# A hybrid encoder block on one core: small products in joint runs, decay rows per head, earlier scan loads, buffers moved by 32 bytes

## The chip, the cores and the metric

The kernel runs on one core of a Trainium2 chip. Its time is the device time of one execution in microseconds. The kernel before took 1745.05 us (median of three runs, 1745.01 to 1745.94).

## The reference

One block with two branches over x of 512 tokens by 2048 features, all in float32. What matters of it, in short:

```python
n = rmsnorm(x, norm_w)
proj = n @ w_in                       # 2048 -> 13376 columns, split into:
# g_qkv, g_z, g_beta, g_a (gated DeltaNet), m_qk, m_v, m_o, m_z, m_i, m_f (mLSTM), gates
# branch A, 8 heads of 128, both directions: conv of width 5 + silu, l2norm of q and k, then by chunks
decay = exp(where(causal, gc[:, None] - gc[None, :], -inf))
sol = triangular_solve(lower(kb @ k.T * decay) + I, [v * beta, kb * exp(gc)])
v_new = u - w @ state                                   # the scan over chunks, one state per head
state = state * exp(g_last) + k_dec.T @ v_new
out = (q * exp(gc)) @ state + (q @ k.T * decay) @ v_new
# branch B, 8 heads of 128, both directions: stabilised mLSTM by chunks, with a running maximum m
c = f * c + i * k.T @ v ; h = (w_inter * q @ c + scores @ v) / max(|den|, exp(-m))
merged = sigmoid(gates_a) * (y_a @ w_branch_gdn) + sigmoid(gates_b) * (y_b @ w_branch_mlstm)
return rmsnorm(x + merged @ w_out, final_norm_w)
```

## The kernel before, in words

**Large products.** Every weight matrix is cut into units. A unit of `w_in` is 128 output columns: two blocks of 24 products of 128x128 by 128x512. Float32 accuracy comes from a split in two parts: ACT casts the raw weights `wr` to `wh` (L168), DVE subtracts to get `wl` (L169), and a block does 16 products that alternate between `nth` and `ntl` (high and low part of the normed input) against `wh`, and 8 of `nth` against `wl`. The input part is the moving operand. SP issues the loads of `wr` (L159), four blocks ahead at most; the splits are two blocks ahead. The units follow each other in a fixed order: k, q and v of eight GDN heads (`gk`, `gq`, `gv`), their gates `gz`, the merge gates `mg0` to `mg27`, five units for each mLSTM head (`m0` to `m4`), `mg28` to `mg31`, then the branch matrices `br` (moving operand `yh` and `yl`, the split branch outputs), then `w_out` (moving operand `wh` and `wl`). 6560 products are large ones.

**Small products.** All else is written as one generator, `master`. After every fourth large product it is advanced by one step (a tick), up to its next `yield`. So the places of the yields decide between which large products the small ones fall on PE. `master` runs `setup` (gate sums, decay), `gdn_pre` for each head (scores `pgm` and transposes `px`, stored to DRAM), `gdn_solve` (a triangular solve on DVE for all heads, then two copies that transpose it on ACT, L570 and L574), the scan `gdn_head` of eight heads, two at a time (`rolling`), `ml_head` for eight heads, and the split of the branch outputs. The 1008 small products are of float32 and take two instructions each, transposes one.

**Order.** Each engine works through a fixed list in order; an instruction that waits holds up what stands behind it. SP issues nearly all transfers, weights and small ones, from one list. In `setup`, the decay of all 16 rows (head times direction) is made at once: one broadcast load of [128, 16, 512], then for each of four column blocks a DVE subtract (L416), two POOL selects (L419) and an ACT Exp (L421). In `gdn_pre`, ACT makes `sqt` (L462) and PE sums it in `pn` (L478). In `gdn_solve`, POOL takes a power `rk` (L523), DVE makes `cvv` (L546) and `brk` (L527) from it, and PE transposes `brk` to `pb` (L531).

**The scan.** `gdn_load` (L583) issues all loads of a head: `hr` (1664 KB), `xt` and `xi` (blocks of the solve), `qg` and `gar`. A head does `pw` twice, then four steps: `kps` (but in the first), `rhs` on DVE, `vps`, `vn` on ACT, `sps`, `sn` on DVE, and the output products `og`.

**Memory.** Pools are stacked from both sides of the on-chip memory; a tile's address follows from the sizes of those before it. The change adds tiles of 8 floats, 32 bytes per partition, at the start of some pools.

Of the kernel before, what the change touches and what calls it, by code (L numbers as in the profile page):

```python
# [13 lines left out]
P = 128  # L14
# [24 lines left out]
def hybrid_block(  # L39
# [55 lines left out]
    st = {}  # L95

# [135 lines left out]
    em = const.tile([P, NT, 16], F32, name="em")  # L232
    mud = const.tile([P, 2, H, 2, NT], F32, name="mud")
# [11 lines left out]
    def setup():  # L245
# [43 lines left out]
        st["dec"] = open_pool("p1").tile([P, 16, T], F32, name="dec")  # L289
        dec = st["dec"]  # L290
# [54 lines left out]

        gct = su.tile([P, NT, 16], F32, name="gct")
# [4 lines left out]
        for t in range(NT):  # L351
# [5 lines left out]
        nc.sync.dma_start(dec.rearrange("p q n -> p (q n)"),  # L357
                          d_gc.rearrange("q n -> (q n)").rearrange("(o n) -> o n", o=1).partition_broadcast(P))
# [70 lines left out]
        open_pool("p1b")  # L429
# [22 lines left out]

    def gdn_pre(h):
        p1b, dec = st["p1b"][1], st["dec"]
        while f"gq{h}" not in done:
            yield
        ckq = st["ckq", h]
        sqt = p1b.tile([P, T], F32, tag="sqt", name=f"sqt{h}")
        sqk = p1b.tile([P, P], F32, tag="sqk", name=f"sqk{h}")
# [4 lines left out]
        la = p1b.tile([P, 2, NT, 2, P], F32, tag="la", name=f"la{h}", bufs=2)  # L464
        for tt in range(2):
            pgm = pp.tile([P, 2, 2, P], F32, tag="mix", name=f"pgm{h}{tt}")
            for i in range(2):
                cs = slice((tt * 2 + i) * P, (tt * 2 + i + 1) * P)
                nc.tensor.matmul(pgm[:, i], ckq[:, 0, cs], ckq[:, :, cs], start=True, stop=True)  # L469
            yield  # L470
            for d in range(2):
                dv = dec[:, d * H + h, tt * 2 * P:(tt + 1) * 2 * P].rearrange("p (t i) -> p t i", i=P)
                nc.vector.tensor_tensor(la[:, d, tt * 2:tt * 2 + 2], pgm,
                                        dv.unsqueeze(2).broadcast_to([P, 2, 2, P]), op=ALU.mult)
            yield
        pn = pp.tile([P, 512], F32, tag="acc", name=f"pn{h}")
        for t in range(NT):
            nc.tensor.matmul(pn[:, t:t + 1], sqt[:, t * P:(t + 1) * P], ones, start=True, stop=True)  # L478
        nc.vector.tensor_copy(ssq[:, h, :], pn[:, 0:4])
        yield  # L480
        px = pp.tile([P, NT, P], F32, tag="mix", name=f"px0{h}")
        for t in range(NT):
            nc.tensor.transpose(px[:, t, :], ckq[:, 0, t * P:(t + 1) * P], ident)
        kv = p1b.tile([P, 2, T], F32, tag="kv", name=f"kv{h}", bufs=2)
        nc.scalar.copy(kv[:, 0, :], px.rearrange("p a b -> p (a b)"))
        for t in range(NT):
            nc.scalar.activation(sqk, px[:, t, :], AF.Square, accum_out=ssk[:, t, h:h + 1])
        dh = d_head[h]
        for a in range(2):
            hs_, os_ = slice(a * 64, a * 64 + 64), slice(64 - a * 64, P - a * 64)  # L490
            for d in range(2):
                nc.sync.dma_start(d_lane[d, h, a::2].rearrange("t j i -> j t i"), la[hs_, d, :, 0, hs_])
            nc.sync.dma_start(dh[hs_, HC_Y:HW].rearrange("p (t i) -> p t i", i=64), la[hs_, a, :, 0, os_])
        nc.sync.dma_start(dh[:, HC_AT:HC_KQ].rearrange("p (d t i) -> p d t i", d=2, i=P), la[:, :, :, 1, :])
        nc.sync.dma_start(dh[:, HC_KQ:HC_Y], ckq.rearrange("p a n -> p (a n)"))
# [5 lines left out]
        px = pp.tile([P, NT, P], F32, tag="mix", name=f"px1{h}")  # L501
        for t in range(NT):
            nc.tensor.transpose(px[:, t, :], cv[:, t * P:(t + 1) * P], ident)
        nc.scalar.copy(kv[:, 1, :], px.rearrange("p a b -> p (a b)"))
        yield
        yield
        nc.sync.dma_start(dh[:, HC_KV:HC_AT], kv.rearrange("p a n -> p (a n)"))
# [6 lines left out]
    def gdn_solve():  # L514
        ln = open_pool("ln")
# [37 lines left out]
        for c in range(1, 63):  # L553
# [15 lines left out]
        li = ln.tile([P, 64, 64], F32, name="li")  # L569
        nc.scalar.copy(li[0:64].rearrange("p m j -> p j m"), lx[0:64])  # L570
# [3 lines left out]
        nc.scalar.copy(li[64:128].rearrange("p m j -> p j m"), l0[64:128])  # L574
        for d in range(2):
            nc.sync.dma_start(lanes(d_inv[d]), li[d * 64:(d + 1) * 64])
        yield
# [3 lines left out]
    half = lambda a: slice(a * 64, a * 64 + 64)  # L581

    def gdn_load(h):  # L583
# [4 lines left out]
        hd = p2.tile([P, HW], F32, tag="hd", name=f"hr{h}", bufs=3)  # L588
        nc.sync.dma_start(hd, d_head[h])
# [5 lines left out]
        qg = p2.tile([P, 2, T], F32, tag="qg", name=f"qg{h}", bufs=3)  # L595
        nc.sync.dma_start(qg, d_egc[h::8].partition_broadcast(P))
        g_a = p2.tile([P, T], F32, tag="gar", name=f"gar{h}", bufs=3)
        nc.sync.dma_start(g_a, d_ga[h])
        st["hl", h] = hd, qg, xt, xi, g_a

    def gdn_head(h):
        p2 = st["p2"][1]
        if h + 1 < H:
            gdn_load(h + 1)
        hd, qg, xt, xi, g_a = st["hl", h]
# [38 lines left out]
        for n in range(NT):  # L644
# [23 lines left out]
            if n < NT - 1:  # L668
                for d, t in enumerate(tiles):
                    sps = pp.tile([P, P], F32, tag=f"st{d}", name=f"sps{h}_{n}_{d}", bufs=1)  # L670
                    nc.tensor.matmul(sps, kd[:, d, t], vn[:, d], start=True, stop=True)  # L671
                    sn = p2.tile([P, P], F32, tag=f"sn{d}", name=f"sn{h}_{n}_{d}", bufs=4)
                    if n == 0:
                        nc.vector.tensor_copy(sn, sps)
                    else:
                        nc.vector.scalar_tensor_tensor(
                            sn, cur[d], egl[:, t, d * H + h:d * H + h + 1], sps, op0=ALU.mult, op1=ALU.add)
                    new[d] = sn
# [63 lines left out]
    def ml_head(h):  # L742
# [6 lines left out]
        for _ in range(4):  # L749
            yield  # L750
        px = pp.tile([P, NT, P], F32, tag="mix", name=f"mpk{h}")
        for t in range(NT):
            nc.tensor.transpose(px[:, t, :], ck[:, t * P:(t + 1) * P], ident)
        ktok = p3.tile([P, NT, P], F32, tag="ktok", name=f"mkt{h}")
        nc.scalar.copy(ktok, px)
# [5 lines left out]
        kw = p3.tile([P, 2, NT, P], F32, tag="kw", name=f"kw{h}")  # L761
        for d in range(2):
            nc.vector.tensor_tensor(kw[:, d], ktok, ksc[:, :, d * H + h:d * H + h + 1].broadcast_to([P, NT, P]),
                                    op=ALU.mult)
            yield
# [452 lines left out]
```

## Time and profile before

| what | value |
|---|---|
| median of three runs | 1745.05 us (1745.01 to 1745.94) |
| the profiled execution's own time | 1745.24 us |
| its span | 1743.4 us |
| PE busy | 1698.1 us, 97% |
| DVE, ACT, POOL busy | 867.7 us (50%), 607.7 us (35%), 86.1 us (5%) |
| chain that ended last | PE 93%, issue 2%, ACT 2%, DMA 1%, DVE 1%, POOL 1% |
| transfers | 243.53 MB, mean 140 GB/s |

A busy time counts how long an engine had at least one instruction at work. The chain is followed back from the last instruction to what released each one, so its shares say which engine's work makes up the time. Times in the timeline are microseconds from the span's start.

### The profile page before, as it was taken

What the parts mean: (1) busy time and instruction counts of PE and PEld (TensorE: products, weight loads), DVE (VectorE), ACT (ScalarE), POOL (GpSimd) and SP (SyncE); (2) the same over time, 40 slices, a digit from 0 to 9 for tenths busy, and PEclk for the clock granted to TensorE, in tenths of its full rate; (3) what the DMA queues carried; (4) which work ended last, traced back from release to release, by engine and by line L of the source; (5) the groups of instructions that cost most, each with busy time, mean ns of one, the idle gap of its engine ahead of it and who ended that gap; (6) DMA issues with size and microseconds to landing.
All of it is one profiled execution on the core that took longest, in us unless ns stands there. A gap on an engine that the chain in (4) does not pass through costs nothing.

```text
span 1743.4 us, 20957 instructions
## 1 busy us (share of the span) xinstructions
PE 1698.1 (97%) x8250; PEld 1406.4 (81%) x8250; DVE 867.7 (50%) x1270; ACT 607.7 (35%) x940; POOL 86.1 (5%) x109
## 2 busy tenths in 40 slices
PE   6979999999999899999999999999999999999998
PEld 6768888878887688888888888888888888888886
DVE  5764555569992544322344545444454444443342
ACT  6553333322234232352343343344334322222231
POOL 1030000010001211010000000000000000000000
PEclk9989999999999999999999999999999999999999
DMA  7655455554459777254433443344334644445232
GB/s 191 202 129 142 131 140 146 147 165 118 114 137 268 210 205 230 80 163 127 109 106 97 112 115 97 103 115 115 85 94 124 205 145 145 140 148 188 96 106 97
DMA packets 325932, 243.53 MB, mean 140 GB/s; under 512 B 38121, under 2 KB 292458, under 8 KB 323530
## 3 DMA queue, kind: packets, MB, share of 16 engines
q1 hardware_dynamic: 324928, 240.49, 48.5%
q8 instruction: 65, 1.06, 0.3%
q10 hardware_dynamic: 905, 1.70, 0.3%
q14 instruction: 34, 0.27, 0.0%
HBM read 203.13 MB, written 38.96 MB: 139 GB/s over the span
## 4 chain that ended last, share of the span: by engine, by line
PE 93%; issue 2%; ACT 2%; DMA 1%; DVE 1%; POOL 1%; SPq 0%; POOLq 0%; DVEq 0%; ACTq 0%
PE pj_m L205 25%; PE pj_mg L205 19%; PE pj_br L205 10%; PE wo L972 9%; PE pj_gv L205 5%; PE pj_gz L205 5%; PE pj_gq L205 4%; PE pj_gk L205 4%; PE og L640 1%; PE vps L663 1%; PE pgm L469 1%; PE ph L804 1%; PE sps L671 1%; PE pj_gk L1092 1%; PE kps L653 1%
## 5 line engine op out<-in xcount | busy, mean ns | idle before, releaser
L169 DVE TENSOR_TENSOR wl<-wr,wh 128x1024 fp32r<-128x1024 f32 x270 | 329.4, 1222 | 455.3 <-ACT wh L168 107.8
L168 ACT CAST wh<-wr 128x1024 fp32r<-128x1024 f32 x270 | 283.9, 1052 | 763.6 <-PE pj_m L205 192.6
L205 PE MATMUL pj_m<-nth,wh 128*128 128x512 f32 x640 | 255.1, 399 | 0.0
L205 PE MATMUL pj_m<-ntl,wh 128*128 128x512 f32 x640 | 249.8, 390 | 0.0
L205 PE MATMUL pj_mg<-nth,wh 128*128 128x512 f32 x512 | 204.2, 399 | 1.5 <-ACT wh L168 1.5
L205 PE MATMUL pj_mg<-ntl,wh 128*128 128x512 f32 x512 | 199.9, 390 | 0.0
L205 PE MATMUL pj_m<-nth,wl 128*128 128x512 f32 x640 | 163.9, 394 | 0.0
L205 PEld LDWEIGHTS pj_m<-ntl,wh 128*128 128x128 f32 x640 | 120.4, 188 | 23.1
L205 PEld LDWEIGHTS pj_m<-nth,wh 128*128 128x128 f32 x640 | 120.3, 188 | 23.0
L205 PEld LDWEIGHTS pj_m<-nth,wl 128*128 128x128 f32 x640 | 117.8, 188 | 22.9
L205 PE MATMUL pj_mg<-nth,wl 128*128 128x512 f32 x512 | 131.2, 394 | 0.0
L205 PEld LDWEIGHTS pj_mg<-nth,wh 128*128 128x128 f32 x512 | 96.3, 188 | 20.6 <-ACT wh L168 1.9
L205 PEld LDWEIGHTS pj_mg<-ntl,wh 128*128 128x128 f32 x512 | 96.3, 188 | 18.5
L205 PEld LDWEIGHTS pj_mg<-nth,wl 128*128 128x128 f32 x512 | 94.4, 188 | 18.9
L205 PE MATMUL pj_br<-yl,wh 128*128 128x512 f32 x256 | 101.5, 396 | 0.0
L205 PE MATMUL pj_br<-yh,wh 128*128 128x512 f32 x256 | 100.7, 394 | 0.0
L972 PE MATMUL wo<-wh,mh 128*128 128x512 f32 x256 | 100.0, 391 | 0.0
L972 PE MATMUL wo<-wh,ml 128*128 128x512 f32 x256 | 99.8, 390 | 0.0
L972 PE MATMUL wo<-wl,mh 128*128 128x512 f32 x256 | 72.9, 390 | 0.0
L937 DVE TENSOR_TENSOR mgr<-pj_br,mgr 128x512 f32<-128x512 f32 x32 | 22.1, 692 | 91.7 <-PE pj_br L205 91.7
L205 PE MATMUL pj_br<-yh,wl 128*128 128x512 f32 x256 | 64.9, 395 | 0.0
L205 PEld LDWEIGHTS pj_br<-yl,wh 128*128 128x128 f32 x256 | 48.0, 188 | 12.0
(320 smaller groups left out, 2562.6 us busy)
## 6 DMA issues: line engine op xcount, KB each, us to landing
wr<-in_w_in_dram SPq DMA_DIRECT2D x206, 512.0 KB, 4.0
wr<-in_w_out_dram SPq DMA_DIRECT2D x32, 512.0 KB, 3.6
hr<-d_head SPq DMA_DIRECT2D x8, 1664.0 KB, 8.1
d_gate<-gt SPq DMA_DIRECT2D x32, 256.0 KB, 2.8
e<-d_row SPq DMA_DIRECT2D x8, 1024.0 KB, 8.1
mgr<-d_gate SPq DMA_DIRECT2D x32, 256.0 KB, 4.3
wr<-in_w_branch_gdn_dram SPq DMA_DIRECT2D x16, 512.0 KB
wr<-in_w_branch_mlstm_dram SPq DMA_DIRECT2D x16, 512.0 KB, 4.1
```

The costliest lines, as they stand in the source:

```text
L168: nc.scalar.copy(hi[:, 0:m], self.raw[:, 0:m])
L169: nc.vector.tensor_tensor(lo[:, 0:m], self.raw[:, 0:m], hi[:, 0:m].bitcast(F32), op=ALU.subtract)
L205: nc.tensor.matmul(ps[0:m, :], l, r, start=(first and n == 0), stop=(last and n == len(jobs) - 1))
L469: nc.tensor.matmul(pgm[:, i], ckq[:, 0, cs], ckq[:, :, cs], start=True, stop=True)
L640: nc.tensor.matmul(po[:, t], l, r, start=not opened, stop=last)
L653: nc.tensor.matmul(kps[:, d], kT[:, cols(t)], cur[d], start=True, stop=True)
L663: nc.tensor.matmul(vps[:, d], xt[:, d, t], rhs[d], start=True, stop=True)
L671: nc.tensor.matmul(sps, kd[:, d, t], vn[:, d], start=True, stop=True)
L804: nc.tensor.matmul(ph, e4[:, d, 0, t, :], vv[:, t, :], start=(n == 0), stop=True)
L937: nc.vector.tensor_tensor(g_, ps, g_, op=ALU.mult)
L972: nc.tensor.matmul(ps, l[:, kt, ts_], r, start=(kt == 0 and l is mh and r is hv), stop=(kt == NK - 1 and r is lv))
L1092: nc.tensor.matmul(pk[:, ts_], w, act[:, kt, ts_], start=not opened, stop=last)
```

## The change

- The decay is no longer made in `setup`. `dec_load` loads two rows of one head, one head ahead, and `gdn_pre` does the subtract, the two selects and the Exp for its head.
- `gdn_pre` issues its scores, the sums `pn` (now in bank `st0`) and both sets of transposes in one run after `gv`; the squares are taken from the copy in SBUF.
- In `gdn_solve`, the two transposing copies become eight, and a pool `p2a` is open for `gdn_load_a` (`hr`, `qg`, `gar`), issued for two heads during the solve. `gdn_load_b` loads `xt` and `xi` after it.
- In `gdn_head`, the states of both directions share one PSUM bank and one tile. `rolling` advances both heads before it yields.
- `ml_head` does the transposes and scores in one run, all six state products in one run, and the eight outputs in one run with three copies.
- Tiles of 32 bytes (`pad`, `pad3`, `padf`) stand at the start of the right side, of `p3` and of `fp`.

```diff
+    pad = ctx.enter_context(pool("pad", side="right"))
+    pad.tile([P, 8], F32, name="pad")
...
-        st["dec"] = open_pool("p1").tile([P, 16, T], F32, name="dec")
-        dec = st["dec"]
+        open_pool("p1")
...
-        nc.sync.dma_start(dec.rearrange("p q n -> p (q n)"),
-                          d_gc.rearrange("q n -> (q n)").rearrange("(o n) -> o n", o=1).partition_broadcast(P))
+        dec_load(0)
...
-        for t in range(NT):
-            dt_ = dec[:, :, t * P:(t + 1) * P]
-            nc.vector.tensor_tensor(dt_, dt_, gct[:, t, :].unsqueeze(2).broadcast_to([P, 16, P]), op=ALU.subtract)
-            for d in range(2):
-                v = dec[:, d * H:(d + 1) * H, t * P:(t + 1) * P]
-                nc.gpsimd.affine_select(out=v, in_=v, pattern=[[0, H], [1 - 2 * d, P]], compare_op=ALU.is_ge,
-                                        fill=-1e30, base=0, channel_multiplier=2 * d - 1)
-            nc.scalar.activation(dt_, dt_, AF.Exp)
-            yield
...
+    def dec_load(h):
+        dec = st["p1"][1].tile([P, 2, T], F32, tag="dec", name=f"dec{h}", bufs=2)
+        nc.sync.dma_start(dec, d_gc[h::8].partition_broadcast(P))
+        st["dec", h] = dec
+
     def gdn_pre(h):
...
+        if h + 1 < H:
+            dec_load(h + 1)
...
+        nc.vector.tensor_tensor(dec4, dec4, g4.broadcast_to([P, 2, NT, P]), op=ALU.subtract)
+        for d in range(2):
+            nc.gpsimd.affine_select(out=dec4[:, d], in_=dec4[:, d], pattern=[[0, NT], [1 - 2 * d, P]],
+                                    compare_op=ALU.is_ge, fill=-1e30, base=0, channel_multiplier=2 * d - 1)
+        for _ in range(3):
+            yield
+        nc.scalar.activation(dec, dec, AF.Exp)
         while f"gq{h}" not in done:
             yield
...
         nc.scalar.activation(sqt, ckq[:, 1, :], AF.Square)
+        while f"gv{h}" not in done:
+            yield
+        cv = st["cv", h]
+        for _ in range(4):
+            yield
+
+        pgm = [pp.tile([P, 2, 2, P], F32, tag="mix", name=f"pgm{h}{tt}") for tt in range(2)]
...
+        pn = pp.tile([P, 8], F32, tag="st0", name=f"pn{h}", bufs=1)
...
+        px = [pp.tile([P, NT, P], F32, tag="acc", name=f"px{i}{h}") for i in range(2)]
...
+            if c in (24, 48):
+                gdn_load_a(c // 24 - 1)
...
+        for d, (to, of) in enumerate(((l0[0:64], lx[0:64]), (lx[64:128], l0[64:128]))):
+            tr = to.rearrange("p m j -> p j m")
+            for q in range(4):
+                js = slice(q * 16, q * 16 + 16)
+                nc.scalar.copy(tr[:, js], of[:, js])
+                yield
+            nc.sync.dma_start(lanes(d_inv[d]), to)
...
+                sps = pp.tile([P, 2, P], F32, tag=f"st{h % 2}", name=f"sps{h}_{n}", bufs=1)
+                sn = p2.tile([P, 2, P], F32, tag="sn", name=f"sn{h}_{n}", bufs=4)
...
                     act.remove(g)
-                    continue
+            for _ in act:
                 yield
...
+        for d in range(2):
+            sps = pp.tile([P, 3, P + 1], F32, tag=f"st{d}", name=f"msp{h}{d}", bufs=1)
+            cd = p3.tile([P, 3, P + 1], F32, tag=f"cn{d}", name=f"cn{h}{d}", bufs=2)
+            cn.append((sps, cd))
+            for n in range(3):
+                t = n if d == 0 else 3 - n
+                nc.tensor.matmul(sps[:, n, :], kw[:, d, t, :], vv[:, t, :], start=True, stop=True)
...
+        for _ in range(4):
+            yield
...
+        for q, (q0, q1) in enumerate(((0, 3), (5, 8), (3, 5))):
+            ph = pp.tile([P, q1 - q0, P + 1], F32, tag=("acc", "acc", "mix")[q], name=f"ph{h}{q}")
...
         yield from gdn_solve()
         open_pool("p2")
-        gdn_load(0)
+        gdn_load_b(0)
+        gdn_load_b(1)
...
+        p3.tile([P, 8], F32, name="pad3")
...
+        fp.tile([P, 8], F32, name="padf")
```

On ACT, around head 0's decay, the kernel before has this (`sqt0` is what `pn` of head 0 needs; the number behind a name is the head, behind `wh` the block):

```order
L168 CAST wh10_986<-wr10_908 128x1024
L434 ACTIVATE ca_g01_977<-pj_gk1_914,cwg_115 128x512
L421 ACT_TABLE_LOAD
L421 ACTIVATE dec_508<-dec_508 128x16x128 x2
L396 ACTIVATE row1_623<-row1_623 8x512
L421 ACTIVATE dec_508<-dec_508 128x16x128
L168 CAST wh11_1017<-wr11_945 128x1024
L421 ACTIVATE dec_508<-dec_508 128x16x128
L168 CAST wh12_1054<-wr12_984 128x1024
L462 ACTIVATE sqt0_811<-ckq0_677 128x512
```

The changed kernel has there:

```order
L442 ACT_TABLE_LOAD
L442 ACTIVATE ckq0_686<-ca_g10_772 128x512
L464 ACT_TABLE_LOAD
L464 ACTIVATE dec0_589<-dec0_589 128x1024
L472 ACTIVATE sqt0_790<-ckq0_686 128x512
L426 ACTIVATE ca_g20_844<-pj_gv0_785,cwg_119 128x512
L398 ACTIVATE row1_627<-row1_627 8x512
L173 CAST wh9_913<-wr9_813 128x1024
L464 ACTIVATE dec1_677<-dec1_677 128x1024
L497 COPY kv0_900<-px00_889 128x512
```

Four Exp of the whole decay stood in front of `sqt0`; now one Exp of head 0's decay does, and head 1's stands behind it.

On SP, at the start of the scan, the kernel before has between `wr85` and `wr86` the loads of heads 0 to 3; the last of them are:

```order
L596 DMA qg2_4002<-d_egc_72 128x2x512
L598 DMA gar2_4004<-d_ga_70 128x512
L703 DMA d_y_77<-yfa0_4217 128x512
L589 DMA hr3_4262<-d_head_69 128x3328
L593 DMA xt3_4259<-d_sol_67 64x4x64 x2
L594 DMA xi3_4264<-d_inv_68 64x4x64
L593 DMA xt3_4259<-d_sol_67 64x4x64 x2
L594 DMA xi3_4264<-d_inv_68 64x4x64
L596 DMA qg3_4271<-d_egc_72 128x2x512
L598 DMA gar3_4273<-d_ga_70 128x512
L904 DMA d_gate_76<-gt8_4286 128x512
L159 DMA wr86_4289<-in_w_in_dram 128x8x128
```

The changed kernel has `wr85`, the `xt` and `xi` loads of heads 0 and 1, and then:

```order
L610 DMA xt2_4087<-d_sol_67 64x4x64 x2
L611 DMA xi2_4090<-d_inv_68 64x4x64
L610 DMA xt2_4087<-d_sol_67 64x4x64 x2
L611 DMA xi2_4090<-d_inv_68 64x4x64
L934 DMA d_gate_76<-gt8_4257 128x512
L164 DMA wr86_4260<-in_w_in_dram 128x8x128
L164 DMA wr87_4321<-in_w_in_dram 128x8x128
L611 DMA xi3_4362<-d_inv_68 64x4x64 x2
L597 DMA qg3_4355<-d_egc_72 128x2x512
```

`hr`, `qg` and `gar` of heads 0 to 2 have gone up, between the weight loads of the solve, and all of head 3 has moved behind `wr87`.

On ACT, around the cast of `wh86`, the kernel before has:

```order
L665 COPY vn2_0_4409<-vps2_0_4406 128x256
L665 COPY vn2_1_4470<-vps2_1_4467 128x256
L665 COPY vn2_2_4548<-vps2_2_4545 128x256
L903 ACTIVATE gt10_4569<-pj_mg10_4420,vec_114 128x512
L665 COPY vn2_3_4608<-vps2_3_4605 128x256
L632 COPY xt3_4259<-pw23_4614 64x4x64
L168 CAST wh86_4416<-wr86_4289 128x1024
```

The changed kernel has:

```order
L680 COPY vn0_0_4029<-vps0_0_4026 128x256
L680 COPY vn0_1_4067<-vps0_1_4064 128x256
L933 ACTIVATE gt10_4522<-pj_mg10_4411,vec_118 128x512
L680 COPY vn0_2_4147<-vps0_2_4144 128x256
L173 CAST wh86_4407<-wr86_4260 128x1024
L173 CAST wh87_4456<-wr87_4321 128x1024
```

The cast stood behind the scan's steps of heads 0 to 2; now it stands behind three steps of head 0.

## Rows read from the trace of the kernel before

**Rows 1.** The page: busy time by engine, and the chain that ended last
```profile
PE 1698.1 (97%) x8250; PEld 1406.4 (81%) x8250; DVE 867.7 (50%) x1270; ACT 607.7 (35%) x940; POOL 86.1 (5%) x109
...
PE 93%; issue 2%; ACT 2%; DMA 1%; DVE 1%; POOL 1%; SPq 0%; POOLq 0%; DVEq 0%; ACTq 0%
```

**Rows 2.** Waits of PE: what waited, releaser, total us, times, longest us
```profile
PE pb L531 <- DVE brk L527: 2.1, 1, 2.1
...
PE pj_mg L205 <- ACT wh L168: 1.5, 1, 1.5
```

**Rows 3.** Windows: length, busy us (instructions) by engine, PEclk, DMA share, GB/s
```profile
97.40:111.70 14.30, 5.56 (x22) 5.08 (x22) 11.46 (x19) 11.85 (x21) 4.49 (x5) 0.64 0.41 99
...
357.30:361.00 3.70, 3.59 (x11) 2.78 (x12) 2.62 (x7) 1.06 (x2) 1.56 (x6) 0.54 0.99 421
...
557.80:608.70 50.90, 41.12 (x343) 34.56 (x343) 24.21 (x62) 11.67 (x39) 12.29 (x14) 0.93 0.82 226
608.70:768.60 159.90, 158.04 (x970) 133.70 (x969) 66.22 (x125) 46.85 (x108) 18.13 (x20) 1.00 0.61 169
```

**Rows 4.** Timeline, 70 to 107 us: start, us, engine, operation [idle before <-releaser]
```profile
73.09 1.28 ACT L450 ACT_TABLE_LOAD   x1
74.38 0.63 ACT L450 ACTIVATE ckq<-ca_g 128x512 f32<-128x512 f32 x1
74.92 0.67 ACT L434 ACTIVATE ca_g<-pj_gv,cwg 128x512 f32<-128x512 f32 x1
...
84.99 16.89 POOL L419 TENSOR_SCALAR_AFFINE_SELECT dec<-dec 128x1024 f32<-128x1024 f32 x8 [53.44 <-PE pj_gk L205]
...
95.65 1.92 ACT L421 ACTIVATE dec<-dec 128x2048 f32<-128x2048 f32 x1 [7.00 <-POOL dec L419]
...
106.23 1.02 PE L478 MATMUL pn<-ones,sqt 128*128 128x1 f32 x4 [8.74 <-ACT sqt L462]
```

**Rows 5.** Groups by line: busy us, mean ns of one | idle before
```profile
L416 DVE TENSOR_TENSOR dec<-dec,gct 128x2048 f32<-128x2048 f32 x4 | 9.1, 2271 | 0.0
...
L523 POOL TENSOR_TENSOR rk<-rk,mhalf 128x32 f32<-128x32 f32 x1 | 5.4, 5445 | 249.6 <-DVE rk L522 249.6
```

**Rows 6.** Timeline of SP's queue: weight loads around the scan's first loads
```profile
534.92 2.06 SPq L159 DMA_DIRECT2D wr<-in_w_in_dram  x1
...
594.81 1.37 SPq L159 DMA_DIRECT2D wr<-in_w_in_dram  x2
```

**Rows 7.** Timeline of PE within the scan, 584 to 589 us
```profile
584.05 0.71 PE L671 MATMUL sps<-vn,kd 128*128 128x128 f32 x4
...
587.12 0.68 PE L615 MATMUL pw<-xi,hr 64*64 64x64 f32 x16
587.73 0.71 PE L671 MATMUL sps<-vn,kd 128*128 128x128 f32 x4
588.28 0.61 PE L640 MATMUL og<-vn,hr 128*128 128x128 f32 x4
588.73 0.42 PE L653 MATMUL kps<-sn,hr 128*128 128x128 f32 x2
```

**Rows 8.** Timeline of PE: low-part products of successive blocks, gate and branch stage
```profile
1357.43 1.98 PE L205 MATMUL pj_mg<-nth,wl 128*128 128x512 f32 x8
...
1362.87 1.98 PE L205 MATMUL pj_mg<-nth,wl 128*128 128x512 f32 x8
...
1384.74 2.03 PE L205 MATMUL pj_br<-yh,wl 128*128 128x512 f32 x8
...
1390.34 2.03 PE L205 MATMUL pj_br<-yh,wl 128*128 128x512 f32 x8
```

**Rows 9.** Timeline of PE: two small runs of an mLSTM head, four large products apart
```profile
944.76 0.38 PE L804 MATMUL ph<-va,e 128*128 128x129 f32 x2
...
946.13 0.39 PE L804 MATMUL ph<-va,e 128*128 128x129 f32 x2
```

**Rows 10.** Groups by line: the steps of `cn`
```profile
L813 DVE SCALAR_TENSOR_TENSOR cn<-cn,mud,msp 128x129 f32<-128x129 f32 x32 | 11.2, 349 | 25.8 <-PE msp L808 25.8
```

More of the change, by code (lines that the diff above doesn't have):

```diff
@@ L232, in hybrid_block @@
     em = const.tile([P, NT, 16], F32, name="em")
+    gct = const.tile([P, NT, 16], F32, name="gct")
     mud = const.tile([P, 2, H, 2, NT], F32, name="mud")
@@ L457, in gdn_pre @@
         ckq = st["ckq", h]
-        sqt = p1b.tile([P, T], F32, tag="sqt", name=f"sqt{h}")
-        sqk = p1b.tile([P, P], F32, tag="sqk", name=f"sqk{h}")
+        sqt = p1.tile([P, T], F32, tag="sqt", name=f"sqt{h}")
+        sqk = p1.tile([P, P], F32, tag="sqk", name=f"sqk{h}")
         for _ in range(4):
@@ L462, in gdn_pre @@
         nc.scalar.activation(sqt, ckq[:, 1, :], AF.Square)
[L464 to L495, printed above, removed]
         while f"gv{h}" not in done:
@@ L573, in gdn_solve, with gdn_load_a, gdn_load_b @@
         nc.sync.dma_start(lanes(d_sol[1]), l0[64:128])
[L574 to L577, printed above, removed]
-        close_pool("ln")
-    half = lambda a: slice(a * 64, a * 64 + 64)
-    def gdn_load(h):
+        for d, (to, of) in enumerate(((l0[0:64], lx[0:64]), (lx[64:128], l0[64:128]))):
[5 more added lines that the diff above has]
+            nc.sync.dma_start(lanes(d_inv[d]), to)
+        close_pool("ln")
+    def gdn_load_a(h):
+        p2a = st["p2a"][1]
+        hd = p2a.tile([P, HW], F32, tag="hd", name=f"hr{h}", bufs=3)
+        nc.sync.dma_start(hd, d_head[h])
+        qg = p2a.tile([P, 2, T], F32, tag="qg", name=f"qg{h}", bufs=3)
+        nc.sync.dma_start(qg, d_egc[h::8].partition_broadcast(P))
+        g_a = p2a.tile([P, T], F32, tag="gar", name=f"gar{h}", bufs=3)
+        nc.sync.dma_start(g_a, d_ga[h])
+        st["hla", h] = hd, qg, g_a
+    def gdn_load_b(h):
         p2 = st["p2"][1]
@@ L668, in gdn_head @@
             if n < NT - 1:
+                sps = pp.tile([P, 2, P], F32, tag=f"st{h % 2}", name=f"sps{h}_{n}", bufs=1)
+                sn = p2.tile([P, 2, P], F32, tag="sn", name=f"sn{h}_{n}", bufs=4)
                 for d, t in enumerate(tiles):
[L670 to L678, printed above, removed]
+                    nc.tensor.matmul(sps[:, d], kd[:, d, t], vn[:, d], start=True, stop=True)
+                if n == 0:
+                    nc.vector.tensor_copy(sn, sps)
+                else:
+                    for d, t in enumerate(tiles):
+                        nc.vector.scalar_tensor_tensor(sn[:, d], cur[d], egl[:, t, d * H + h:d * H + h + 1],
+                                                       sps[:, d], op0=ALU.mult, op1=ALU.add)
+                new = [sn[:, 0], sn[:, 1]]
             for d, t in enumerate(tiles):
@@ L748, in ml_head @@
         ck = st["m", 0, h]
-        for _ in range(4):
+        for _ in range(6):
             yield
[L751 to L755, printed above, removed]
         e4 = e.rearrange("p d b (n i) -> p d b n i", i=P)
@@ new lines, in ml_head @@
+        for t in range(NT):
+            nc.tensor.transpose(pv_[:, t, :], cvt[:, t * P:(t + 1) * P], ident)
+        for t in range(NT):
+            cs = slice(t * P, (t + 1) * P)
+            nc.tensor.matmul(psc[:, t, :], ck[:, cs], cq[:, cs], start=True, stop=True)
+        ktok = p3.tile([P, NT, P], F32, tag="ktok", name=f"mkt{h}")
+        nc.scalar.copy(ktok, pk_)
+        vv = va[:, h % 2]
+        nc.scalar.copy(vv[:, :, 0:P], pv_)
+        kw = p3.tile([P, 2, NT, P], F32, tag="kw", name=f"kw{h}")
@@ new lines, in ml_head @@
+        for n in range(3):
+            for d, (sps, cd) in enumerate(cn):
+                t = n if d == 0 else 3 - n
+                if n == 0:
+                    nc.vector.tensor_copy(cd[:, 0, :], sps[:, 0, :])
+                else:
+                    nc.vector.scalar_tensor_tensor(cd[:, n, :], cd[:, n - 1, :], mud[:, d, h, 1, t:t + 1],
+                                                   sps[:, n, :], op0=ALU.mult, op1=ALU.add)
+        for _ in range(4):
+            yield
+        hr = p3.tile([P, 2, NT, P + 1], F32, tag="hr", name=f"hr{h}")
@@ new lines, in ml_head @@
+        hrf = hr.rearrange("p d t c -> p (d t) c")
+        for q, (q0, q1) in enumerate(((0, 3), (5, 8), (3, 5))):
+            ph = pp.tile([P, q1 - q0, P + 1], F32, tag=("acc", "acc", "mix")[q], name=f"ph{h}{q}")
+            for j in range(q0, q1):
+                d, t = j // NT, j % NT
+                n = t if d == 0 else 3 - t
+                if n > 0:
+                    nc.tensor.matmul(ph[:, j - q0, :], e4[:, d, 1, t, :], cn[d][1][:, n - 1, :], start=True, stop=False)
+                nc.tensor.matmul(ph[:, j - q0, :], e4[:, d, 0, t, :], vv[:, t, :], start=(n == 0), stop=True)
+            nc.scalar.copy(hrf[:, q0:q1, :], ph)
```

105 lines of the change are left out of this document (51 added, 54 removed).

## The prediction

> **What bounds the kernel now.** I read the page first. TensorE is busy for 97% of the span and the chain of waits is 93% PE [rows 1], so the time is the sum of what PE issues plus the few places where it stands still or runs slowly. An edit is worth only what it takes out of that sum, and work that it removes from DVE, ACT or POOL is worth nothing unless PE waits for it there. Then I read the waits of PE, where two entries lie in stages that the change rewrites [rows 2], and after them the windows: four stretches in which PE's clock is below 1.0 or in which PE works off few instructions for their time [rows 3]. Last, the timeline gives prices: two starts of the same row, one block of 24 large products apart, give the pace of a stage [rows 8], and the small products of the scan give theirs [rows 7].
>
> The profiled execution spans 1743.4 us and took 1745.24 us, 0.2 us above the median of 1745.05 us, so changes worked out inside it may be taken from 1745.2 directly. All small and large products stay (1008 and 6560 in either order); what can change is waiting, pace and the number of runs.
>
> **Head 0's decay.** Now PE stands still for 8.74 us before head 0's `pn`, which needs `sqt`. ACT works in order, and in front of `sqt` stand four Exp of 128x2048 at 1.9 us each, which wait for eight POOL selects that take 16.89 us together [rows 4]. When PE resumes, its clock is at half until 111.7: the window shows 0.64 on average, and the 5.4 us from 106.23 to 111.7 hold work for 2.7 us [rows 3, 4]. The stall therefore costs 8.7 + 2.7 = 11.4 us. Afterwards the same place has one subtract of 128x1024 (half of 2271 ns, so 1.1 us [rows 5]), two selects of 128x512 (half of 16.89/8, so 1.06 us each) and one Exp of some 1.0 us; they can start as soon as the broadcast of 512 KB has landed, while `ckq` for head 0 is ready near 75.0. ACT has then a table load of 1.28 us [rows 4], the Exp and `sqt` to do: ready near 78. `gv0` ends before 74.92, when ACT first reads it [rows 4]; the joint run comes four ticks later, with the current one 20 large products of 0.227 us, so near 79.5. What is late next is `cv0`: on ACT it stands behind the copy and the four squares of that run's first half, and I find it ready about 1 us before PE needs it. I take -11.4 us; the other end is 0 if another decay comes in the way (a rival below). For later heads nothing is counted: PE's waits name no other wait of this stage, and each decay is loaded a whole head ahead (three units of 48 x 0.227 us, 33 us).
>
> The trace shows the first activation 1.29 us after a table load began [rows 4]. The Trainium skill (ScalarE: Activation LUTs, "What ACT_TABLE_LOAD costs") speaks against this part: it prices each switch at a load of about 1.28 us and a drain of about 1.38 us. The trace agrees with the load and shows no drain behind it; by the page's estimate the two loads ahead of `sqt` would bring it to about 80.8, and the stall would come back with 0.7 us, which makes the sum 0.7 us worse.
>
> **The start of the solve.** `pb` waits 2.06 us for `brk` [rows 2], and the clock then is 0.54 in the 3.7 us after [rows 3], so 1.7 us more. DVE does `cvv` before `brk`, and `cvv` waits for a POOL power of 5.45 us [rows 5]. This order is kept, but the last head's four `la` products (0.68 us each) and the squares now come directly before it rather than well before: by adding up the chain, `brk` is ready 12.7 us after the last joint run begins, and PE arrives after 9.0 us. The wait grows from 2.1 to 3.7 us. With some more half clock I take +2.0 us (bounds: 0, if PE comes no earlier, and +4).
>
> **The end of the solve.** The one wait for a cast, 1.5 us [rows 2], comes from two long ACT copies ahead of it. Eight quarter copies in the same queue with no cast between them are the same work: +0.3 us, between -1.5 and +1.5.
>
> **The scan of the GDN heads.** This is the largest term. From 557.8 to 608.7 PE issues 343 small instructions and no large one [rows 3]. Of them about 126 are 64 wide at 0.61/16 = 0.038 us, and 217 are 128 wide at 0.45/4 = 0.1125 us [rows 7], together 29.2 us; 21.7 us are lost to latencies between the dependent steps and to half clock (0.93). The reason stands on SP: between the weight loads at 534.92 and 594.81 [rows 6] come the loads of four heads, some of which wait for earlier heads to finish, so PE has no weights for `pj_mg11` and nothing to put between the scan's steps. In the next window, 970 instructions are 480 large ones (108.8 us at 0.2267) and 490 small ones (45.4 us) against 159.9 us: 5.7 us lost. Altogether 27 us.
>
> Afterwards the large parts of heads 0 to 2 are issued during the solve, and only 18 small loads stand between `wr85` and `wr86`. Now some 38 transfers take the 60 us between the two [rows 6], 1.6 us each with their waits for earlier heads; 18 would take 29 us at that rate, and as they wait for no head I take half of it, 15 us. From the issue of `wr85` PE has work up to 557.8, 23 us, so `wr86` is then in time or nearly so. What stays: on ACT the cast `wh86` still stands behind `vn0_2`, so head 0's second and third step are done with no large product between. One such step takes 587.73 - 584.05 = 3.7 us now, of which 2.8 us are products [rows 7], so 1 us per step is lost, plus 1 to 2 us for the cast, 1.4 us for the first chain of head 0 (its links of 1.2 to 1.9 us get 3 to 6 large products as cover) and some more for heads 2 to 7: 7 to 10 us remain. I take -17 us. The bounds are -22 (only the cast's wait remains) and -8 (PE again runs out of weights for part of three heads).
>
> **Alignment.** In the m and gate stages one block of 24 takes 1362.87 - 1357.43 = 5.44 us, in the branch stage 1390.34 - 1384.74 = 5.60 us [rows 8]: 226.7 against 233.3 ns per product, with the same shapes and no wait. What differs is the moving operand. Adding up the tiles of each pool, `yh` and `yl` start at 32 modulo 64 bytes in the kernel before, `nth`, `ntl` and the split weights at 0; the pads of 32 bytes put `yh` and `yl` at 0. If that is the cause, 768 x 6.6 ns = -5.1 us; if not, 0. The pad in `fp` moves the last five blocks' split weights, which are the moving operand of 120 products in the output stage, from 0 to 32: +0.8 us by the same price. I take -4.3 us. Nothing is counted for DVE or ACT, which PE does not wait for.
>
> Those rows show two paces for one shape. The Trainium skill (SBUF: "SBUF — State Buffer", Door 1) names cachelines of 16 bytes as the unit in which crossing costs, and 32 modulo 64 is on such a boundary, so by that page alignment would change nothing; the trace neither agrees nor disagrees, since no run here has the same stage at another address.
>
> **Fewer runs.** 224 runs of small products become 148. Four small products between large ones take 946.13 - 944.76 - 4 x 0.2267 = 0.46 us [rows 9], against 0.45 us for four inside a long run [rows 7]: 10 to 17 ns per run, so 76 x 0.016 = -1.2 us (bounds 0 and -4, if the dearer first runs go). In the ML heads the gain needs its waits hidden: `kw` is ready 2.7 us after the transposes and wanted after 4.6; `cn` has six DVE steps of 0.35 us [rows 10] with one weight split between them and is ready at 8.7 us against 9.6. No wait, but with under 1 us to spare.
>
> **Sum:** -11.4 + 2.0 + 0.3 - 17 - 4.3 - 1.2 = -31.6, so 1745.2 - 31.6 = 1713.6 us; I say 1714.
>
> **Rivals.**
> (B) *The branch stage is slow for another reason*, such as its alternation of `yh` and `yl`. For it: no row has the stage aligned. Against it: `nth` and `ntl` alternate too, at the faster pace. Then the 4.3 us are not won: 1718. By the skill's page on SBUF named above it would come out so.
> (C) *The scan stays a chain.* PE is given the steps of one head back to back, since casts wait behind `vn` on ACT and loads behind each other on SP; the early loads move the gap by a block rather than close it. For it: the order of ACT at `wh86`. Against it: the transfers that wait for a head's end are gone from between the loads. Only 8 us are won: 1723.
> (D) *The change does not do what it says for head 0:* the second head's decay, whose load is issued one head ahead, puts its Exp in front of `cv0` on ACT, and PE waits there instead. With the same price, 11.4 us: 1725.
> (E) *Slower: joint runs wait for the last of their inputs.* At the eight ML heads, a run that needed one `cn` step now needs all six. If the convolution's DVE work (four steps of 0.75 us) falls into that chain, `ph` is late by 2.2 us, and the half clock that follows such a pause, as after `pb`, adds 1.7 us: 3.9 us per head, 31 us in all, 1745; with `msp` late for the same reason as well, 1750 or more. It decides from 4 us per head. Against it: DVE's order has only one split in that chain, and PE had no wait in this stage.
>
> **How the numbers follow.** Forecast 0.52, B 0.20, C 0.14, D 0.08, E 0.06. About 0.2% (3.5 us) is what a measurement of this kernel can tell from no change; of E half is slower than that, the rest is divided. So faster 0.94, same 0.02, slower 0.04. The forecast's own range, from its terms' bounds, is 1706 to 1721; the range for 8 times in 10 reaches to C and D: 1706 to 1726.
>
> **What would show it.** Right: no wait of `pn`; no half clock near 106; a wait of `pb` of 3 to 5 us; large products among the scan's steps, and under 10 us lost there; 5.44 us per block in the branch stage; no PE wait in the ML heads. Wrong: `px1` waiting for `cv0` (D); a stretch of over 25 us without large products near 558 (C); 5.60 us per block in the branch stage (B); entries for `msp` or `ph` in PE's waits (E).

## The result, and the profile after

The changed kernel took 1718.78 us (median of four runs, 1718.46 to 1719.93) against 1745.03 us: a ratio of 0.985 (95% interval 0.9833 to 0.9867), 26.3 us less. The forecast was 1714 us, the range 1706 to 1726 us.

The page after, busy time and chain (as [rows 1]):

```profile
PE 1679.7 (98%) x8250; PEld 1404.3 (82%) x8250; DVE 871.2 (51%) x1266; ACT 620.3 (36%) x922; POOL 89.6 (5%) x117
...
PE 86%; DVE 8%; issue 3%; ACT 1%; DMA 1%; POOL 0%; SPq 0%; POOLq 0%; DVEq 0%; ACTq 0%
```

PE does the same work in less time. But DVE, 1% of the chain of waits before, is 8% now. The waits of PE say where it comes in (as [rows 2]):

```profile
PE pj_mg L210 <- ACT wh L173: 8.8, 1, 8.8
PE pv L1114 <- DMA v<-in_gdn_norm_w_dram: 8.3, 1, 8.3
PE pb L538 <- DVE rk L554: 3.5, 1, 3.5
```

The wait of `pn` is gone, the wait of `pb` has grown as forecast, and the cast wait, 1.5 us before, is 8.8 us. The windows of head 0, of the 4 us behind `pb`, of the end of the solve and of the longest stretch without a large product (columns as in [rows 3]):

```profile
74.00:92.00 18.00, 18.00 (x90) 15.17 (x89) 14.32 (x24) 14.93 (x25) 3.21 (x4) 1.00 0.67 176
...
345.00:349.00 4.00, 4.00 (x11) 3.10 (x10) 1.62 (x2) 0.60 (x1) 0.00 (x0) 0.52 0.73 288
...
521.00:530.30 9.30, 0.47 (x3) 0.04 (x1) 0.02 (x1) 9.25 (x8) 0.20 (x1) 0.79 0.90 215
556.80:565.60 8.80, 8.12 (x69) 6.84 (x68) 3.89 (x12) 3.23 (x5) 0.00 (x0) 1.00 0.00 0
```

Head 0 runs without a pause at full clock. In the 4 us behind `pb` the granted clock is about half (0.52). At the solve's end PE is idle for nearly 9 us while ACT is busy throughout. The stretch without large products is 8.6 us long, where it was 50.8. On SP, `wr85` and `wr86` now stand 18 us apart, where it was 60 [rows 6]:

```profile
529.75 2.12 SPq L164 DMA_DIRECT2D wr<-in_w_in_dram  x1
547.80 1.10 SPq L164 DMA_DIRECT2D wr<-in_w_in_dram  x2
```

In the branch stage the low-part products of successive blocks are 5.44 us apart, where it was 5.60 [rows 8]:

```profile
1362.50 1.98 PE L210 MATMUL pj_br<-yh,wl 128*128 128x512 f32 x8
1367.94 1.98 PE L210 MATMUL pj_br<-yh,wl 128*128 128x512 f32 x8
```

Since all large products kept their order, the difference between the starts of the same block in the two traces gives each stage its share:

| stage | forecast | measured |
|---|---|---|
| startup | 0 | -0.4 |
| head 0's decay | -11.4 | -12.1 |
| joint runs of heads 1 to 7 | part of -1.2 | -2.4 |
| start of the solve (`pb`) | +2.0 | +2.4 |
| end of the solve (cast) | +0.3 | +9.1 |
| scan | -17 | -15.9 |
| mLSTM heads | part of -1.2 | -2.9 |
| branch and output stage | -4.3 | -4.4 |
| sum | -31.6 | -26.6 |

One term is wrong by 8.8 us, and the joint runs gave four times their forecast. The two rows of the solve also change from one execution to the next, with the half clock behind each wait: in the traces of e1, e7, e8 and e10 below, which have the changed kernel's code there and the same waits (3.5 us, and 8.8 to 8.9), the row of `pb` comes to -0.2 to +2.4 us and that of the cast to 10.1 to 10.8 us.

### The profile page after: what moved, and what is told of

The parts are those of the page before. It is cut to its first block, busy times and chain, and to the rows that moved or that the text cites. A ratio compares the mean times of both kernels' runs of the same rounds, so it can differ in the third digit from the quotient of the medians.

```text
span 1716.8 us, 20890 instructions
## 1 busy us (share of the span) xinstructions
PE 1679.7 (98%) x8250; PEld 1404.3 (82%) x8250; DVE 871.2 (51%) x1266; ACT 620.3 (36%) x922; POOL 89.6 (5%) x117
## 4 chain that ended last, share of the span: by engine, by line
PE 86%; DVE 8%; issue 3%; ACT 1%; DMA 1%; POOL 0%; SPq 0%; POOLq 0%; DVEq 0%; ACTq 0%
PE pj_m L210 25%; PE pj_mg L210 14%; PE pj_br L210 10%; PE wo L1003 10%; PE pj_gq L210 5%; PE pj_gv L210 5%; PE pj_gk L210 4%; DVE tm L564 2%; DVE lx L567 2%; DVE wl L174 2%; PE og L655 1%; PE pj_gz L210 1%; PE vps L678 1%; PE ph L841 1%; PE pgm L482 1%
## 5 line engine op out<-in xcount | busy, mean ns | idle before, releaser
L174 DVE TENSOR_TENSOR wl<-wr,wh 128x1024 fp32r<-128x1024 f32 x270 | 333.1, 1235 | 452.7 <-ACT wh L173 120.6
L210 PE MATMUL pj_m<-nth,wh 128*128 128x512 f32 x640 | 251.1, 392 | 0.0
L567 DVE TENSOR_TENSOR lx<-lx,tm 128x62 f32<-128x62 f32 (+30 forms) x62 | 56.3, 908 | 1.6
```

The lines of the kernel that those rows point to most:

```text
L174: nc.vector.tensor_tensor(lo[:, 0:m], self.raw[:, 0:m], hi[:, 0:m].bitcast(F32), op=ALU.subtract)
L210: nc.tensor.matmul(ps[0:m, :], l, r, start=(first and n == 0), stop=(last and n == len(jobs) - 1))
L567: nc.vector.tensor_tensor(lx[:, 0:c, c + 1:64], lx[:, 0:c, c + 1:64], tv, op=ALU.add)
```

## The experiments

All are compared with the changed kernel, 1718.8 us, e6 with the kernel before. The kernel before took 1744.6 to 1746.0 us beside them (ratios are to it).

**e1, the pads alone undone.**

```diff
-    pad = ctx.enter_context(pool("pad", side="right"))
-    pad.tile([P, 8], F32, name="pad")
...
-        p3.tile([P, 8], F32, name="pad3")
...
-        fp.tile([P, 8], F32, name="padf")
```

> The changed kernel without its three 32-byte tiles, so yh and yl start at 32 modulo 64 again and the last output blocks at 0. Alignment theory (A): the branch stage goes back to 5.60 us per block of 24, 768 x 6.6 ns = 5.1 us, less 0.4 us in the output stage: 1718.8 + 4.7 = 1723.5 us. Rival (B, the pace comes from something else in the rewritten program): 5.44 us per block stays, 1718.8 us.

1723.8 us, ratio 0.9877 (0.9861 to 0.9894). The branch stage went back to the old pace, 5.60 us per block, and the other stages of large products kept theirs:

```profile
1367.40 2.03 PE L208 MATMUL pj_br<-yh,wl 128*128 128x512 f32 x8
1373.00 2.03 PE L208 MATMUL pj_br<-yh,wl 128*128 128x512 f32 x8
```

**e11, the same cost put where it was not.** One more such tile ahead of `nth` and `ntl`.

```diff
+    ntp.tile([P, 8], F32, name="padn")
     nth = ntp.tile([P, NK, T], F32R, name="nth")
```

> The changed kernel with one more tile of 32 bytes ahead of nth and ntl, so the moving operand of all w_in products (4992) starts at 32 modulo 64. Theory (a start at 32 modulo 64 costs 6.6 ns per product of 512 columns, whatever the stage): +33 us, of which the cast wait at the solve's end takes back about 5: 1747 us, 5.60 us per block in the gate stage. Rival (only the branch stage is open to it): 1718.8 us.

1742.3 us, ratio 0.9979 (0.9968 to 0.9991). Now the gate stage takes 5.60 us per block and the branch stage behind it 5.44:

```profile
1369.95 2.03 PE L211 MATMUL pj_mg<-nth,wl 128*128 128x512 f32 x8
1375.55 2.03 PE L211 MATMUL pj_mg<-nth,wl 128*128 128x512 f32 x8
...
1386.66 1.98 PE L211 MATMUL pj_br<-yh,wl 128*128 128x512 f32 x8
1392.11 1.98 PE L211 MATMUL pj_br<-yh,wl 128*128 128x512 f32 x8
```

With e1 this settles the cause of the two paces: the start of the moving operand, not the stage. The weights start at the same addresses in e11 as in the changed kernel, and `yh` and `yl` do too. The sum, +23.6 us, is 4.4 us below the 33 us less 5 us expected: the cast wait fell from 8.8 to 4.3 us, as expected, and the blocks with small products among them rose by less than from 5.44 to 5.60.

**e2, POOL's products after the solve.** With the early loads, POOL's products `qg` of heads 0 to 2 had moved into the solve as well.

```diff
+            ms = nc.gpsimd.memset(xt[half(1 - d), d, :, half(d)], 0.0)
+        st["ms", h] = ms.ins if hasattr(ms, "ins") else ms
...
+            with tc.issue_after(st["ms", h]) if h < 3 else ExitStack():
                 nc.gpsimd.tensor_tensor(qg[:, d, :], qg[:, d, :], qT, op=ALU.mult)
```

> The changed kernel with POOL's products qg of heads 0 to 2 ordered behind the memsets of xt, so after the solve. Theory (DVE's solve sets when the cast wh82 comes, and POOL's products stretch solve steps on DVE from 0.4 to 1.4 us): the solve's steps sum to 106.4 us and not 110.5, the cast wait falls from 8.8 to about 4.7 us, 1718.8 - 4.1 = 1714.7 us. Rival (the eight copies on ACT set the wait whenever they come, or the stretch has another cause): the wait stays near 8.8 us, 1718.8 us; if the late products delay the scan, 1720.

1711.9 us, ratio 0.9808 (0.9793 to 0.9822): 6.9 us less than the changed kernel, more than expected. First the changed kernel, steps of the solve on DVE around such a product, then e2 at the same steps:

```profile
372.74 0.34 DVE L567 TENSOR_TENSOR lx<-lx,tm 128x180 f32<-128x180 f32 x1
372.85 2.80 POOL L639 TENSOR_TENSOR qg<-qg,hr 128x512 f32<-128x512 f32 x2 [30.18 <-DMA d_ga<-ga]
373.11 1.38 DVE L564 TENSOR_TENSOR tm<-lx 128x236 f32<-128x236 f32 x1
374.53 1.37 DVE L567 TENSOR_TENSOR lx<-lx,tm 128x236 f32<-128x236 f32 x1
```

```profile
371.94 0.40 DVE L564 TENSOR_TENSOR tm<-lx 128x236 f32<-128x236 f32 x1
372.38 0.41 DVE L567 TENSOR_TENSOR lx<-lx,tm 128x236 f32<-128x236 f32 x1
```

A step of 0.40 us takes 1.38 us beside the POOL product. From its first product to its last step the solve takes 154.0 us in the changed kernel and 148.1 in e2; the steps proper account for 4.1 of the 5.9 us, the splits `wl` between them for 1.1. The cast wait fell from 8.8 to 3.4 us, which is 5.4 us. The rest is half clock: e2's trace has none behind the shorter cast wait, and a shorter spell of it behind `pb`, where the edit changes nothing. The Trainium skill ("SBUF — State Buffer", the section "SBUF: two separate sides") has the rule that a POOL operation and a DVE operation with two inputs in SBUF take a shared pair of ports one at a time. The trace agrees: the two long steps end at 374.49 and 375.90 us, just behind the two POOL products of 1.40 us each that begin at 372.85. The forecast had not looked for it.

**e3 and e4, an earlier start of the solve.** The solve's two first products stood behind `wl54` and `ga1` on DVE, which wait for PE; e3 puts them ahead, e4 adds e2's edit.

```diff
+            with tc.issue_after(st["lxi"]) if n == 54 else ExitStack():
                 nc.vector.tensor_tensor(lo[:, 0:m], self.raw[:, 0:m], hi[:, 0:m].bitcast(F32), op=ALU.subtract)
...
+            with tc.issue_after(st["lxi"]) if h == 1 else ExitStack():
                 nc.vector.tensor_scalar(ga, ga, gnw_c, None, op0=ALU.mult)
```

> The changed kernel with the two products that begin the solve on DVE ahead of wl54 and ga1, which wait for PE. Theory: the solve begins near 354 in place of 359.9 us and ends 5.7 us earlier, the cast wait falls from 8.8 to 3.1 us: 1718.8 - 5.7 = 1713.1 us. Rival (the solve's pace, not its start, is bound by what PE and ACT give DVE in between): the end moves under 2 us, 1717 to 1719.

> Both edits, the solve's start ahead of wl54 and ga1 and POOL's products after the solve. Theory (one chain through DVE, the two delays add): 9.8 us are taken from a wait of 8.8 us, so the wait goes and no more: 1718.8 - 8.8 = 1710 us, 1709.5 to 1711.5. Rival (the two delays overlap): no better than the better of the two alone, 1713.

1719.6 and 1716.0 us: this theory fell. In e3 the first product starts 7.2 us earlier than in the changed kernel (first line), but ACT's copies behind the last step start only 0.8 us earlier (513.89 in the changed kernel):

```profile
359.90 4.41 DVE L549 TENSOR_TENSOR lx<-l,bsc 64x4096 f32<-64x4096 f32 x1
```

```profile
352.72 4.41 DVE L550 TENSOR_TENSOR lx<-l,bsc 64x4096 f32<-64x4096 f32 x1
```

```profile
513.10 7.54 ACT L587 COPY l<-lx 64x1024 f32<-64x1024 f32 x4 [10.01 <-DVE lx L569]
```

The steps share DVE with 28 splits `wl` and other products in a fixed order, two of which now stand behind the solve's start. The time won at the front is spent within: DVE idles 9.1 us inside the solve in place of 3.2, 3.7 of them before a `ga`, which waits for ACT, and 2.4 before a split, which waits for PE. e4 is 4.1 us slower than e2 alone, and its cast wait is 5.5 us against e2's 3.4: the new order costs time and wins none.

**e5, the copies on DVE as well.** e2, and

```diff
-                nc.scalar.copy(tr[:, js], of[:, js])
+                nc.vector.tensor_copy(tr[:, js], of[:, js])
```

> The changed kernel with POOL's qg products after the solve (as in e2) and the eight transposing copies on DVE in place of ACT. Theory (the 3.4 us of cast wait that e2 left come from the copies ahead of the casts on ACT): wh82 is cast in time, DVE's copies take about 9 us after the solve's end near 507 and wl82 follows near 519, PE is there at 520: the wait goes, 1711.9 - 3.4 = 1708.5 us. Rival (a transposing copy is as slow on DVE, 15 us for the eight): wl82 comes near 525, 1.5 us late, 1710.5 us.

1706.3 us, ratio 0.9781 (0.9767 to 0.9794). The cast wait is gone. That is 5.6 us below e2 where 3.4 were expected; 1.6 us of it lie behind `pb`, where e5's trace happens to have no half clock. On ACT, four copies took 7.60 us; on DVE they take half, and the splits follow without a gap:

```profile
513.89 7.60 ACT L585 COPY l<-lx 64x1024 f32<-64x1024 f32 x4 [9.46 <-DVE lx L567]
521.51 7.09 ACT L585 COPY lx<-l 64x1024 f32<-64x1024 f32 x4
528.63 0.69 ACT L933 ACTIVATE gt<-pj_mg,vec 128x512 f32<-128x512 f32 x1
529.22 2.94 ACT L173 CAST wh<-wr 128x1024 fp32r<-128x1024 f32 x3
```

```profile
508.41 3.91 DVE L585 COPY l<-lx 64x1024 f32<-64x1024 f32 x4
512.35 3.90 DVE L585 COPY lx<-l 64x1024 f32<-64x1024 f32 x4
516.28 3.50 DVE L174 TENSOR_TENSOR wl<-wr,wh 128x1024 fp32r<-128x1024 f32 x3
```

The first fence is the changed kernel, where the three casts stand behind eight copies; the second is e5. The edit takes the copies out of the casts' way and halves their time at once, so what each of the two is worth is not shown.

**e6, the decay per head alone.** `dec_load` and the decay code of the change in the kernel before, nothing else.

> The kernel before with the decay made per head as in the change, and nothing else of it. Theory (the return at the solve's end comes from POOL's early products, not from the earlier start): head 0's stall goes, 12.5 us, the solve moves along with PE and its wait stays near 1.5 us: 1744.6 - 12.5 = 1732 us. Rival (any lead won ahead of the solve is given back at its end, since the solve ends by its own time): half or more is given back, 1738 to 1743 us.

1734.8 us, ratio 0.9945 (0.9932 to 0.9957): 10.4 us less than the kernel before, nearer to the theory's 12.5 than to the rival's range. Its cast wait is that of before:

```profile
PE pj_mg L205 <- ACT wh L168: 1.5, 1, 1.5
```

Here the solve's first product starts 11.8 us earlier than before, and its end comes 11.8 us earlier too. So a lead that PE wins ahead of the solve is not lost at its end as such; 11.8 us are still there behind the cast, and 1 us goes in the scan.

**e7, the mLSTM heads of before** in the changed kernel.

> The changed kernel with the mLSTM heads of before (runs of two to eight products). Theory (joint runs save 0.3 us per head there, as the stage differs between the two traces): 1718.8 + 2.4 = 1721 us. Rival (14 us per thousand runs, as forecast: 56 runs by 0.016 us): 1719.7 us.

1722.1 us, 3.3 us more. One head's period, from one `mpo` to the next, is 61.58 us in the kernel before, 61.21 in the changed one and 61.63 in e7, in this order:

```profile
908.64 0.60 PE L850 MATMUL mpo<-ident,hs 128*128 128x128 f32 x4
...
970.22 0.60 PE L850 MATMUL mpo<-ident,hs 128*128 128x128 f32 x4
```

```profile
889.04 0.60 PE L878 MATMUL mpo<-ident,hs 128*128 128x128 f32 x4
...
950.25 0.60 PE L878 MATMUL mpo<-ident,hs 128*128 128x128 f32 x4
```

```profile
889.75 0.60 PE L866 MATMUL mpo<-ident,hs 128*128 128x128 f32 x4
...
951.38 0.60 PE L866 MATMUL mpo<-ident,hs 128*128 128x128 f32 x4
```

The excess time around each kind of small run, that is what the starts of the large products there are apart beyond 0.2267 us each, tells in the same traces where the gain lies. The 48 fewer runs of states and outputs save 0.5 us in all eight heads, near the rival's price; the 16 fewer runs of transposes and scores save 2.4 us.

**e8 to e10, what fills the scan.** e8 issues the loads late in the code but leaves `p2a` open; e9 puts them in `p2`, which opens after the solve; e10 puts the yield back in `rolling`.

```diff
-            if c in (24, 48):
-                gdn_load_a(c // 24 - 1)          # e8, e9
...
-        open_pool("p2a")                         # e9
...
-            for _ in act:
-                yield                            # e10: a yield after each head's step
```

> The changed kernel with all loads of a scan head at their old place, after the solve, and one head ahead only. Theory (the early loads fill the scan, but their products on POOL hold up the solve): no cast wait beyond 3.4 us, -7 us, but PE runs out of weights within the scan again, +16 us: near 1728 us. Rival (advancing both heads per tick is what filled the scan): the scan stays as in the changed kernel, 1712 us.

> The changed kernel without the pool p2a: hr, qg and gar of the scan lie in p2 again, which opens only after the solve (in e8 the pool was still open early and the loads of the first heads still went into the solve). Theory (place for the loads during the solve is what fills the scan): POOL's products leave the solve, -7 us, but 27 loads in place of 18 stand between wr85 and wr86, with three of 1664 KB, wr86 comes 10 to 15 us late: 1724 us. Rival (advancing both heads per tick, kept here, fills the scan): 1712 us.

> The changed kernel with rolling as before: a yield after each head's step, so two heads' steps come two ticks apart and not in one. Theory (the early loads fill the scan): within 2 us of the changed kernel, 1718.8 to 1721 us. Rival (the joint runs of two heads are what filled it): back to the losses of before, 1730 us or more.

e8 took 1717.9 us and told nothing on its question: 18 loads stand between `wr85` and `wr86` as in the changed kernel, and the loads of heads 0 to 2 still go out during the solve, since the order of the program places a transfer where its memory is free, and it was. e9 took 1725.6 us, 13.7 us above e2, which also has POOL's products after the solve. In it SP issues three `hr` ahead of `wr86`, which comes 37 us after `wr85` (first line), and PE has no large product for 35.9 us:

```profile
523.24 2.10 SPq L164 DMA_DIRECT2D wr<-in_w_in_dram  x1
...
529.92 0.34 SPq L592 DMA_DIRECT2D hr<-d_head  x1
539.75 0.34 SPq L592 DMA_DIRECT2D hr<-d_head  x1
549.43 0.33 SPq L592 DMA_DIRECT2D hr<-d_head  x1
560.38 1.02 SPq L164 DMA_DIRECT2D wr<-in_w_in_dram  x2
```

```profile
547.20:583.10 35.90, 26.87 (x217) 22.00 (x216) 16.95 (x38) 7.99 (x22) 7.34 (x7) 0.90 0.66 191
```

e10 took 1716.6 us, no slower than the changed kernel, and its longest stretch without a large product is 8.6 us as well. The joint advance of two heads is worth nothing that these runs can tell; the place for early loads is worth the 13.7 us.

**e12, the best version.** e5, and `cvv` behind `brk` on DVE:

```diff
+        bki = nc.vector.tensor_tensor(brk, beta4, bc(rk2), op=ALU.mult)
...
+        with tc.issue_after(bki):
+            nc.vector.tensor_tensor(cvv, beta4, bc(rk), op=ALU.mult)
```

> e5 (copies on DVE, qg products after the solve) and brk ahead of cvv on DVE, so that pb does not wait for POOL's power. Theory: the wait of pb, 3.5 us, and the half clock behind it go, and nothing gives it back since the solve's end no longer holds PE: 1706.3 - 4.7 = 1701.6 us. Rival (the solve's end becomes the bound again and returns it): 1706 us.

1701.4 us, ratio 0.9743 (0.9728 to 0.9759), 17.4 us below the changed kernel. `brk` is done before `cvv` waits for POOL, and `pb` finds it:

```profile
337.51 0.22 DVE L534 TENSOR_TENSOR brk<-tgs,rk 128x64 f32<-128x64 f32 x1
342.82 0.22 DVE L555 TENSOR_TENSOR cvv<-tgs,rk 128x64 f32<-128x64 f32 x1 [5.09 <-POOL rk L530]
```

## Why the prediction was right, and where not

The time lay in the range and the way was right, but the step "The end of the solve" failed: it said that eight quarter copies with no cast between them "are the same work: +0.3 us, between -1.5 and +1.5", and the traces show +9.1. The copies are the same work, but they begin when DVE's solve ends, and that was not carried along. The solve's first product and the first copy in the kernel before (those of the changed kernel stand under e3 and e5):

```profile
366.55 4.41 DVE L542 TENSOR_TENSOR lx<-l,bsc 64x4096 f32<-64x4096 f32 x1
...
518.49 7.61 ACT L570 COPY li<-lx 64x4096 f32<-64x4096 f32 x1 [1.58 <-DVE lx L560]
```

PE came to the solve 12.5 us earlier than before. DVE began it only 6.7 us earlier and took 154.0 us for it and not 151.9, so it ended 4.6 us earlier. PE's wait grew by 7.3 us; the rest of the 9.1 us is half clock behind the longer wait (the granted clock is 0.50 from 530.3 to 533.2 us, and 1.00 from 535.4 to 538.3 us in the kernel before). The text had read the 1.5 us of wait as an amount, when it meant that DVE's chain of solve, copies and cast already set PE's time there: what PE wins ahead of it counts only as far as the chain's end moves too. In e6 that end moves with PE, and nothing is lost.

e2 and e5 show what held the chain up: POOL's products, by 5.9 us of the solve's length, and the eight copies on ACT ahead of the casts, by the remaining 3.4 us of wait. The part of the prediction on the scan had moved the loads into the solve without counting what they release: two POOL products per head. Of the growth, 5.4 us of wait are shown to be POOL's. That the solve began only 6.7 us earlier for PE's 12.5 is seen in the trace, but e3 could not turn it into time, so the share of the late start stays open.

Head 0 came as forecast (-12.1), and D did not happen: `px` did not wait, and ACT's queue at head 0 had the decay of head 1 behind `sqt`. In the changed kernel the two table loads there begin at 72.67 and 74.61 us and the activations behind them at 73.96 and 75.91, 1.29 and 1.30 us later, as in [rows 4]. So the drain that the Trainium skill (ScalarE: Activation LUTs, "What ACT_TABLE_LOAD costs") prices did not appear.

The start of the solve came near its forecast (+2.4 for +2.0), with a wait of 3.5 us for the 3.7 worked out. e12 shows that the wait hangs on the order `cvv`, `brk`; that it grew for the reason given is not tested apart. Part of the 2.4 us is chance: in e1, with the same wait, the window behind `pb` runs at full clock, where the changed kernel has 0.52, and the stage is 2.6 us shorter:

```profile
345.00:349.00 4.00, 4.00 (x20) 3.27 (x19) 1.50 (x2) 0.95 (x2) 0.00 (x0) 1.00 0.77 310
```

In the scan the size was right (-15.9 for -17) with the cause given: e9 against e2 shows 13.7 us for the loads' place. In the branch stage alignment came as forecast (5.44 us per block for 5.60), and e1 and e11 refute B; the unit of 16 bytes in the Trainium skill ("SBUF — State Buffer", Door 1) does not explain it. At the end of the output stage the same price did not hold: the pads move the split weights of the last five blocks from 0 to 32 modulo 64, which was to cost 0.8 us, and the starts of the large products in the changed kernel and in e1 show 0.3. Why is not known.

The runs were mis-sized: 0.016 us for each of 76 made 1.2 us, and 5.3 were won. The price fits the states and outputs (48 fewer runs, 0.5 us), from which it was taken; transposes and scores, on their own before and in one run now, gave more per run (16 fewer, 2.4 us, in the mLSTM heads; 28 fewer runs of transposes, scores and sums, 2.4 us, in heads 1 to 7 of `gdn_pre`). The bound of -4 named that case and was too small as well. E did not happen: no wait of `msp` or `ph`.

That the sum came within 5 us of the forecast is in part luck: the 8.8 us that the solve's end cost too much and the 4.1 us that the runs gave too much run against each other. It came out at B's 1718 us for another reason than B's.

## What to carry to other kernels

A short wait of the busiest engine can be the tip of a chain on another engine: before counting a gain ahead of it, ask what moves the chain's end. When loads are moved earlier, follow what they release, since an engine in order starts work as soon as its data is there, and that work may share ports with another's. A start at a multiple of 64 bytes for the moving operand is worth checking by the pace of one stage against another of the same shape.

## What the hardware showed that was not expected

- A moving operand of 512 float32 columns that starts at 32 modulo 64 bytes costs 233.3 ns per product and not the 226.7 of a start at 0: in the branch stage by the change and e1, in the gate stage by e11. In the last five blocks of the output stage the same move cost 0.3 us and not the 0.8 of that price.
- Behind the same wait of 3.5 us, the granted clock of the next microseconds was 0.52 in one execution and 1.00 in another (the changed kernel and e1), worth 2.6 us.
- DVE's product of two SBUF inputs took 1.38 us beside a POOL product, and 0.40 without one (the changed kernel and e2).
- A transposing copy of 64x1024 took 1.9 us on ACT and 0.98 on DVE (the changed kernel and e5).
